# Last norm's vector turned through DRAM on GpSimd's queue, two constants loaded from GpSimd, and the first half's output in four pieces with banks of their own

## The chip, the cores and the metric

The kernel runs on one core of a Trainium2 chip. The metric is the device time of one execution in microseconds (us). The core has five engines with queues of their own: TensorE (PE, with its weight loads as PEld), VectorE (DVE), ScalarE (ACT), GpSimd (POOL) and SyncE (SP). Queues of SP, ACT and POOL also issue DMAs (in the profile SPq, ACTq and POOLq), which 16 DMA engines carry out. Matmul results land in PSUM, which has 8 banks of 128 x 512 numbers.

## What is computed

One decoder layer on 256 tokens of width 1024, in float32, with a final norm:

```python
mod = silu(c) @ w_ada + b_ada                       # 9 vectors of 1024: shifts, scales, gates
u = modulate(rmsnorm(h, norm_ff1), sh1, sc1)
h = h + 0.5 * g1 * swiglu(u, w_ff1_gate, w_ff1_up, w_ff1_down)
u = modulate(rmsnorm(h, norm_mix), sh2, sc2)
h = h + g2 * token_mixing(u, ...)                   # gated linear attention beside causal attention
u = modulate(rmsnorm(h, norm_ff2), sh3, sc3)
h = h + 0.5 * g3 * swiglu(u, w_ff2_gate, w_ff2_up, w_ff2_down)
return rmsnorm(h, norm_final)

def rmsnorm(x, g):
    return x * rsqrt(mean(x * x, axis=-1) + EPS) * g
```

The hidden width is 2816. The attention of the mixing stage adds a bias by distance, taken from a table `rel_bias` of 4 heads x 32 numbers.

## The kernel before

**Layout.** The activations `h` lie turned: features on the 128 partitions, in 8 blocks, tokens in the free dimension. All weights are loaded as 128 x 1024 pieces (512 KB) into 8 buffers called `raw` (line 186). Each piece is split into a rounded part `hi` (by ACT) and the rest `lo` (by DVE), 6 buffers each (line 193), and each product takes three matmuls (line 236). Nearly all matmuls are therefore of one form, 128 x 128 by 128 x 256.

**Stages.** First the *lead* (lines 327 to 775): the small vectors `colt` (line 328) and the input `x` are loaded, the input's norm is found (a root on POOL, line 425), and the first 32 pieces of weights come from one array, `in_first`, in the order of `LOADS` (line 25): for each of 8 blocks two pieces of the conditioning's weights, for DVE's dot products, and two of the first network's. Then the first feed-forward network, with the constants of the mixing stage loaded in between (`mix_constants`, line 793, at the fourth step); then the mixing stage, the second feed-forward network (line 1251), and the end (line 1260 on).

**Orders.** The order of ACT, DVE and PE is the order of the code (`in_order`, line 348), since each instruction is chained to the one before it on its engine. SP's and POOL's instructions aren't chained. Waits on data and on buffers are put in when the program is built.

**The constants of the mixing stage.** `mix_constants` loads `tri` into a `raw` buffer, then `mask` (128 x 448 integers), `rel` (the table of biases, 4 x 32) and `wlr_raw` (96 x 256), all from SP (line 796). On POOL, lines 803 to 807 fill a row `rrow` with a constant, copy 16 numbers of `rel` into it, and 16 more stretches (`BUCKETS`). Line 808 writes it to DRAM (`rdram`), and line 809 reads it back as `bias`, 128 x 4 x 256 numbers. `mask` and `bias` are used in the mixing stage.

**The two rows of gains.** The last two of the 8 feature blocks are computed with tokens on the partitions (`straight`), so the end needs two vectors as rows on all partitions. The gate's (`mods[:, 8, 6:8]`) is written from SBUF columns to DRAM on POOL's queue (`gdram`, line 1256), transposing on the way, and read back onto 128 partitions. The final norm's (`nf_row`, line 1258) is read from the end of `in_first`, where its 256 numbers stand as a row, by SP, into a buffer of `gqk`. `nf_row` is used at line 1320 alone.

**The end.** For each half `t` of the tokens `straight_products(t)` gives the last 256 columns; `summed(t)` adds up the squares of the first six blocks (a matmul with a column of ones), `squared(t)` (ACT) those of the last two, `root(t)` (DVE, then POOL) forms one over the root. `turn_out(t)` transposes six blocks of `h` into two banks, and `scaled` multiplies a piece by the root and issues its output: DVE's pieces of 256 columns from SP, ACT's pieces of 512 columns from ACT itself. `scaled_straight(t)` does the last 256 columns on DVE.

Of the kernel before, what the change touches and what calls it, by code (L numbers as in the profile page):

```python
# [10 lines left out]
F32 = mybir.dt.float32  # L11
F32R = mybir.dt.float32r
I32 = mybir.dt.int32
AF = mybir.ActivationFunctionType
ALU = mybir.AluOpType

P = 128
S = 256
D = 1024
# [54 lines left out]
TURNED, STRAIGHT = [0, 4, 2, 1, 5, 3], slice(6 * P, D)  # L74
# [13 lines left out]
C_BADA, C_N1, C_NM, C_N2, C_NF, C_C, C_GN = 0, 72, 80, 88, 96, 104, 112  # L88
# [3 lines left out]
def _places():  # L92

    places, at = {}, 0
    for piece in ["cols", "x0", "x1"] + LOADS.split():
        width = N_COLS if piece == "cols" else D + 2 if piece[0] == "a" else D
        places[piece] = at, width
        at += P * width
    places["nf"] = at, 2
    return places  # L100


FIRST = _places()


@with_exitstack
def hybrid_layer(ctx: ExitStack, tc: tile.TileContext, first, xT, tri_d, mask_d, rel_bias,
                 wlr, ada, gu1, dn1, win, gv, mv, gbr, wout, gu2, dn2, out):
    nc = tc.nc
# [5 lines left out]
    dr = ctx.enter_context(tc.tile_pool(name="dr", bufs=1, space=bass.MemoryType.DRAM))  # L115
# [24 lines left out]
    vec, act, ten = InOrder(nc.vector), InOrder(nc.scalar), InOrder(nc.tensor)  # L140
# [11 lines left out]
    def bank():  # L152
        return pp.tile([P, 512], F32, tag="b", name=name("b"), bufs=8)
# [15 lines left out]
    def row(shape=(P, S), dt=F32, tag="r1", bufs=6):  # L169
        return wk.tile(list(shape), dt, tag=tag, name=name(tag), bufs=bufs)  # L170

    def blk(i):
        return slice(i * P, (i + 1) * P)
# [618 lines left out]

    def mix_constants():
        ctri = load(tri_d)
        for to, src in ((mask, mask_d), (rel, rel_bias), (wlr_raw, wlr)):
            nc.sync.dma_start(to, src)
        act.activation(tri.rearrange("p a c -> p (a c)"), ctri[:, :4 * S], AF.Copy)

        act.activation(wlr_s, wlr_raw, AF.Copy)
        vec.tensor_tensor(out=wlr_s[64:96], in0=wlr_raw[64:96], in1=wlr_s[64:96], op=ALU.subtract)  # L800
        bank()

        nc.gpsimd.memset(rrow, NEG)
        nc.gpsimd.tensor_copy(rrow[:, 127:143], rel[:, :16])
        for bucket, first, last in BUCKETS:
            nc.gpsimd.tensor_copy(rrow[:, 127 + first:128 + last],
                                  rel[:, bucket:bucket + 1].to_broadcast([4, last - first + 1]))
        nc.gpsimd.dma_start(rdram, rrow)
        nc.gpsimd.dma_start(bias, bass.AP(tensor=rdram.tensor, offset=rdram[:, :].offset,
                                          ap=[[1, P], [NREL, 4], [1, S]]))  # L810

        vec.memset(glt.bitcast(F32), 0.0)
        vec.memset(glt[:, :, 16:81:64].bitcast(F32), 1.0)
# [419 lines left out]
    def first_product(i):  # L1233
# [3 lines left out]
        else:  # L1237
# [2 lines left out]
    play(START2, {"A": stream.more, "t": both_gates, "i": normed_part, "s": first_silu, "m": first_product,  # L1240
                  "r": lambda i: hid.add_rows(m[i], i), "o": lambda: low_last(sb[1], S, stream.take(), u3),
                  "g": lambda: next(steps), "H": lambda: rests.append(stream.high()), "L": lambda: rests.pop(0)()})
    def broadcast(src, at):
        t = row(tag="rbs" if at is None else "gqk", bufs=1 if at is None else 4)
        offset = src[:, :].offset if at is None else src.offset + at
        (nc.gpsimd if at is None else nc.sync).dma_start(t, bass.AP(tensor=src.tensor, offset=offset,
                                                                    ap=[[0, P], [1, 2 * P]]))
        return t

    dbanks = []  # L1250
    for at, (what, n) in enumerate(work2[3:-1]):
        pipe.run(gate_up(hid, u3) if what == "f" else down(n, dbanks, hid))
        slabs.step(Q3_AT.count(at))
        if at == 19:
            gdram = dr.tile([2, P], F32, name="gdram")
            nc.gpsimd.dma_start(gdram.rearrange("i p -> p i"), mods[:, 8, 6:8])
            stream.gains = broadcast(gdram, None)
            nf_row = broadcast(first, FIRST["nf"][0])

    bd = Boundary(8, h, lambda j: colt[:, C_NF + j:C_NF + j + 1], added=6, eps=D * EPS / P, order=TURNED)  # L1260
    bd.banks = dbanks
# [23 lines left out]
                    yield mm(b[:, :S], b, rows[:, i, r, blk(t)], ws_[i][part][:, wblk(6).start:wblk(7).stop],  # L1285
                             stop=(rows is hid.tiles[-1] and part == 1 and i == 1))

    ps, rs, cols = [bank(), bank()], [None, None], row((P, 8), tag="tiny", bufs=4)

    def summed(t):  # L1290
        part = bd.rms.parts[0]
        ten.matmul(ps[t][:, 0:1], part[:, blk(t)], ones[:, 0:1], start=True, stop=True)

    def squared(t):
        act.activation(row(tag="sq", bufs=4), straight[t][:, :S], AF.Square, scale=D ** -0.5, accum_out=cols[:, t:t + 1])

    def root(t):
        ms = row((P, 8), tag="tiny", bufs=4)
        vec.scalar_tensor_tensor(ms[:, :1], ps[t][:, 0:1], 1.0 / D, cols[:, t:t + 1], op0=ALU.mult, op1=ALU.add)
        rs[t] = inverse_root(ms, 1)  # L1300

    o = big().rearrange("p k s -> p (k s)")
    turned_o = {}

    def turn_out(t):
        turned_o[t] = [bank(), bank()]
        for j in (4, 5, 0, 1, 2, 3):
            ten.transpose(turned_o[t][j // 4][:, blk(j % 4)], h[:, j, blk(t)], ident)

    def scaled(engine, t, at, n):  # L1310
        src, dst = turned_o[t][at // 512][:, at % 512:at % 512 + n], o[:, t * D + at:t * D + at + n]
        if engine is act:
            act.activation(dst, src, AF.Copy, scale=rs[t][:, 0:1])
        else:
            vec.tensor_scalar(dst, src, rs[t][:, 0:1], None, op0=ALU.mult)
        (nc.scalar if engine is act else nc.sync).dma_start(out[blk(t), at:at + n], dst)  # L1316

    def scaled_straight(t):
        dst = o[:, t * D + 6 * P:(t + 1) * D]
        vec.scalar_tensor_tensor(dst, straight[t][:, :S], rs[t][:, 0:1], nf_row, op0=ALU.mult, op1=ALU.mult)  # L1320
        nc.sync.dma_start(out[blk(t), STRAIGHT], dst)

    all_of(straight_products(0))
    squared(0)
    for at, _ in enumerate(straight_products(1)):
        if at == 2:
            summed(0)
    root(0)
    squared(1)
    summed(1)  # L1330
    scaled_straight(0)
    turn_out(0)
    turn_out(1)
    scaled(vec, 0, 512, 256)
    root(1)
    scaled(act, 0, 0, 512)
    scaled_straight(1)
    scaled(vec, 1, 512, 256)
    scaled(act, 1, 0, 512)

def _c(a):
# [41 lines left out]
def _packed(i):  # L1385
    w = {k: np.asarray(v) for k, v in i.items()}
    d = {}
    x, pieces = _c(w["x"][0]), {}
    d["xT"] = _c(x.T.reshape(KD, P, S).transpose(1, 0, 2).reshape(P, KD * S))
    vec = [w["b_ada"][0], w["norm_ff1"][0], w["norm_mix"][0], w["norm_ff2"][0], w["norm_final"], w["c"][0],  # L1390
           w["gla_norm"][0]]
    pieces["cols"] = np.concatenate(vec).reshape(N_COLS, P).T
    pieces["x0"], pieces["x1"] = x[:P], x[P:]
    d["tri"], d["mask"] = _constants()
    d["rel_bias"] = _c(w["rel_bias"])
    d["wlr"] = np.zeros((3, 32, 256), np.float32)
    d["wlr"][:, :17] = np.concatenate([w["w_gla_lr"][0], w["b_gla_lr"]], 0)
    d["wlr"] = d["wlr"].reshape(96, 256)
    rows = w["w_ada"][0].T.reshape(9, KD, P, D)
    more = np.zeros((2, KD, P, 2), np.float32)  # L1400
    more[:, :, :, 0] = w["b_ada"][0].reshape(9, KD, P)[:2]
    more[1, :, :, 1] = 1.0
    adal = np.concatenate([rows[:2], more], 3)[::-1].transpose(1, 0, 2, 3)
    d["ada"] = _units(rows[2:].reshape(7 * KD, P, D))
    for n in ("1", "2"):
        g, u = (_col_tiles(w[f"w_ff{n}_{x}"][0]) for x in ("gate", "up"))
        both = np.stack([g, u], 2)
        if n == "1":
            lead = both[:LEAD].transpose(3, 1, 0, 2, 4).reshape(KD, P, 2, D)
            both = both[LEAD:]  # L1410
        d["gu" + n] = _c(both.reshape(len(both), P, 2048))
        d["dn" + n] = _row_units(w[f"w_ff{n}_down"][0])
    for k in range(KD):
        for i in range(2):
            pieces[f"a{k}{i}"], pieces[f"l{k}{i}"] = adal[k, i], lead[k, :, i]
    pieces["nf"] = w["norm_final"][6 * P:]
    d["first"] = np.concatenate([pieces[piece].reshape(-1) for piece in FIRST])
    wi = w["w_in"][0]
    at = np.cumsum([0, 256, 256, 512, 16, 512, 512, 512, 512, 1024, 1024])
    gq, gk, gv, glr, gog, mq, mk, mv, ga, gb = (wi[:, a:b] for a, b in zip(at[:-1], at[1:]))  # L1420
    d["win"] = _units(_col_tiles(np.concatenate([gk, gq, mk, mq, gog, ga], 1)))
    for n, m in (("gv", np.concatenate([gv, glr], 1)), ("mv", mv)):
        d[n] = _c(m.reshape(2, 4, P, -1).transpose(0, 2, 1, 3).reshape(2, P, -1))
    br = np.concatenate([_col_tiles(w["w_br_gla"][0]), _col_tiles(w["w_br_moba"][0])], 2)
    d["gbr"] = _c(np.stack([_col_tiles(gb), br], 2).reshape(KD, P, 2 * D))
    d["wout"] = _row_units(w["w_out"][0])
    return d
# [25 lines left out]
```

## Time and profile before

| what | value |
|---|---|
| three timed runs, median (lowest to highest) | 558.63 us (558.34 to 558.64) |
| the profiled execution | 559.21 us |
| its span, first to last instruction | 557.0 us |
| mean granted TensorE clock | 0.998 |
| instructions | 11698 |
| HBM read, written | 140.19 MB, 1.06 MB |

Times in views of the trace are microseconds from the start of the span. The profile is of one execution, so sums are made against its own time; it stands 0.58 us above the median of the timed runs. A row of a view by time gives start, length, engine, line of the kernel, operation, what is written and read by the program's names (`b` stands for several: PSUM banks and the large activations), and in brackets how long the engine sat idle before it, with what ended that. Most operations have line 132, which is a helper that issues them.

### The profile page before, as it was taken

How to read it: one execution, taken by the hardware profiler on the slowest of the kernel's cores; microseconds unless marked ns; L12 is line 12 of the kernel's file. 1: busy time of each engine (PE TensorE's matmuls, PEld its weight loads, DVE VectorE, ACT ScalarE, POOL GpSimd, SP SyncE). 2: the span in 40 equal slices, each digit the busy share in tenths (PEclk: the TensorE clock that was granted, in tenths of full speed). 3: DMA queues.
4: the chain of work that ended last, by engine and by line, in shares of the span. 5: the costliest groups of instructions: out<-in, count | busy, mean ns of one | idle time of the engine just before them, and what ended most of it. 6: DMA issues, size and time to landing. Idle time of an engine off the chain costs nothing.

```text
span 557.0 us, 11698 instructions
## 1 busy us (share of the span) xinstructions
PE 548.8 (99%) x4704; PEld 542.5 (97%) x4704; DVE 443.1 (80%) x695; ACT 305.3 (55%) x509; POOL 16.6 (3%) x37
## 2 busy tenths in 40 slices
PE   7999999999999999999999999999999999999996
PEld 5999999999999999999999999999999999999996
DVE  5999897788887897799998979899975556665555
ACT  5557754443445568953864543587554454455424
POOL 1000030000000100000001000000000000000000
PEclk9999999999999999999999999999999999999999
DMA  8999699999998626454589878834896566797102
GB/s 323 409 408 408 252 342 381 404 354 334 329 352 311 229 76 222 162 192 146 181 289 402 293 260 268 298 137 132 297 343 211 193 216 220 223 215 248 59 1 77
DMA packets 40750, 142.01 MB, mean 255 GB/s; under 512 B 4724, under 2 KB 6616, under 8 KB 40696
## 3 DMA queue, kind: packets, MB, share of 16 engines
q1 hardware_dynamic: 40008, 139.55, 70.4%
q10 hardware_dynamic: 432, 1.05, 0.5%
q8 instruction: 37, 0.61, 0.4%
q0 software_dynamic: 256, 0.66, 0.4%
q14 instruction: 17, 0.14, 0.1%
HBM read 140.19 MB, written 1.06 MB: 254 GB/s over the span
## 4 chain that ended last, share of the span: by engine, by line
PE 97%; DMA 2%; ACT 0%; SPq 0%; issue 0%; ACTq 0%
PE b L132 97%; DMA raw<-in_first 2%; ACT b L132 0%; SPq L190 0%; ACT hi L132 0%; SPq L331 0%; SPq L328 0%; ACTq L1316 0%; ACTq L132 0%
## 5 line engine op out<-in xcount | busy, mean ns | idle before, releaser
L132 PE MATMUL b<-ub,hi 128*128 128x256 f32 (+1 forms) x1920 | 318.5, 277 | 0.6 <-ACT hi L132 0.6
L132 PEld LDWEIGHTS b<-ub,hi 128*128 128x128 f32 x1920 | 280.7, 188 | 1.0 <-ACT hi L132 0.8
L132 DVE TENSOR_TENSOR lo<-raw,hi 128x1024 fp32r<-128x1024 f32 (+2 forms) x190 | 225.3, 1211 | 56.6 <-ACT hi L132 56.0
L132 PE MATMUL b<-ub,lo 128*128 128x256 f32 (+1 forms) x960 | 244.8, 277 | 0.0
L132 ACT ACTIVATE hi<-raw 128x1024 fp32r<-128x1024 f32 (+2 forms) x190 | 193.6, 1045 | 66.6 <-issue 29.9
L132 PEld LDWEIGHTS b<-ub,lo 128*128 128x128 f32 x960 | 170.9, 188 | 0.0
L132 PE MATMUL b<-s,hi 128*128 128x256 f32 x944 | 161.9, 276 | 0.0
L132 PEld LDWEIGHTS b<-s,hi 128*128 128x128 f32 x944 | 142.2, 188 | 0.0
L132 PE MATMUL b<-s,lo 128*128 128x256 f32 x472 | 130.3, 276 | 0.0
L132 PEld LDWEIGHTS b<-s,lo 128*128 128x128 f32 x472 | 88.6, 188 | 0.0
L132 DVE SCALAR_TENSOR_TENSOR raw<-raw,cact 128x1024 f32<-128x1024 f32 (+1 forms) x64 | 75.8, 1220 | 0.1
L132 ACT ACTIVATE s<-m 128x256 fp32r<-128x256 f32 x52 | 21.5, 417 | 81.6 <-DVE m L132 81.4
L132 ACT ACTIVATE sg<-b 128x256 f32<-128x256 f32 x46 | 17.3, 380 | 47.8 <-PE b L132 46.8
L132 DVE TENSOR_TENSOR s<-m,s 128x256 fp32r<-128x256 f32 x52 | 21.9, 424 | 20.6 <-ACT s L132 20.3
L132 DVE TENSOR_TENSOR m<-sg,b 128x256 f32<-128x256 f32 x43 | 17.8, 417 | 12.6 <-ACT sg L132 12.5
L132 ACT ACTIVATE s<-b 128x512 f32<-128x512 f32 (+5 forms) x38 | 14.7, 436 | 17.3 <-PE b L132 16.5
L132 PE MATMUL b<-hi,ub 128*128 128x264 f32 (+1 forms) x96 | 16.7, 323 | 0.0
L132 PEld LDWEIGHTS b<-hi,ub 128*128 128x128 f32 x96 | 13.9, 188 | 1.2
L425 POOL TENSOR_TENSOR tiny<-tiny,mhalf 128x2 f32<-128x2 f32 (+2 forms) x6 | 6.0, 1000 | 233.7 <-DVE tiny L132 233.7
L132 ACT ACTIVATE sq<-b 128x256 f32<-128x256 f32 x24 | 9.1, 405 | 6.3 <-DVE b L132 4.2
L132 DVE SCALAR_TENSOR_TENSOR b<-b,mods,b 128x256 f32<-128x256 f32 x24 | 10.3, 476 | 2.7 <-PE b L132 2.7
L132 ACT ACTIVATE ub<-n,mods 128x256 fp32r<-128x256 f32 x16 | 7.8, 508 | 8.0 <-DVE n L132 8.0
(141 smaller groups left out, 286.0 us busy)
## 6 DMA issues: line engine op xcount, KB each, us to landing
raw<-in_gu SPq DMA_DIRECT2D x72, 512.0 KB, 5.8
raw<-in_ada SPq DMA_DIRECT2D x56, 512.0 KB, 5.5
raw<-in_dn SPq DMA_DIRECT2D x44, 512.0 KB, 6.6
raw<-in_win SPq DMA_DIRECT2D x24, 512.0 KB, 4.4
raw<-in_first SPq DMA_DIRECT2D x16, 513.0 KB, 7.9
raw<-in_first SPq DMA_DIRECT2D x16, 512.0 KB, 7.8
raw<-in_gbr SPq DMA_DIRECT2D x16, 512.0 KB, 6.6
raw<-in_wout SPq DMA_DIRECT2D x8, 512.0 KB, 6.0
```

The costliest lines, as they stand in the source:

```text
L132: x = getattr(self.engine, op)(*args, **kw)
L425: nc.gpsimd.tensor_tensor(out=rs[:, :n], in0=ms[:, :n], in1=mhalf[:, :n], op=ALU.pow)
```

## The change

The final norm's two columns leave the array of the first loads; they are now written from `colt` in SBUF to DRAM and read back as a row, both on POOL's queue, by a function that also serves the gate's columns. `wlr_raw` is loaded by SP directly behind `tri`; `mask` and `rel` are loaded from POOL's queue. At the end both sums of squares share a bank; `turn_out` takes groups of blocks and gives each a bank of its own; ACT scales the first half's four blocks in two pieces of 256 columns, whose outputs SP issues; the first half's blocks 4 and 5 are turned ahead of the second half's sum, and the first half's sum comes two products earlier.

```diff
-    places["nf"] = at, 2
...
-        for to, src in ((mask, mask_d), (rel, rel_bias), (wlr_raw, wlr)):
-            nc.sync.dma_start(to, src)
+        nc.sync.dma_start(wlr_raw, wlr)
+        for to, src in ((mask, mask_d), (rel, rel_bias)):
+            nc.gpsimd.dma_start(to, src)
...
-    def broadcast(src, at):
-        t = row(tag="rbs" if at is None else "gqk", bufs=1 if at is None else 4)
-        offset = src[:, :].offset if at is None else src.offset + at
-        (nc.gpsimd if at is None else nc.sync).dma_start(t, bass.AP(tensor=src.tensor, offset=offset,
-                                                                    ap=[[0, P], [1, 2 * P]]))
+    def as_row(src, tag, bufs):
+        there, t = dr.tile([2, P], F32, name=f"{tag}_dram"), row(tag=tag, bufs=bufs)
+        nc.gpsimd.dma_start(there.rearrange("i p -> p i"), src)
+        nc.gpsimd.dma_start(t, bass.AP(tensor=there.tensor, offset=there[:, :].offset, ap=[[0, P], [1, 2 * P]]))
         return t
...
         if at == 19:
-            gdram = dr.tile([2, P], F32, name="gdram")
-            nc.gpsimd.dma_start(gdram.rearrange("i p -> p i"), mods[:, 8, 6:8])
-            stream.gains = broadcast(gdram, None)
-            nf_row = broadcast(first, FIRST["nf"][0])
+            stream.gains = as_row(mods[:, 8, 6:8], "rbs", 1)
+            nf_row = as_row(colt[:, C_NF + 6:C_NF + 8], "gqk", 4)
...
-    ps, rs, cols = [bank(), bank()], [None, None], row((P, 8), tag="tiny", bufs=4)
+    ps, rs, cols = bank(), [None, None], row((P, 8), tag="tiny", bufs=4)
...
-    def turn_out(t):
-        turned_o[t] = [bank(), bank()]
-        for j in (4, 5, 0, 1, 2, 3):
-            ten.transpose(turned_o[t][j // 4][:, blk(j % 4)], h[:, j, blk(t)], ident)
+    def turn_out(t, *parts):
+        for js in parts:
+            b = bank()
+            for i, j in enumerate(js):
+                ten.transpose(b[:, blk(i)], h[:, j, blk(t)], ident)
+            place[t, js] = b[:, :len(js) * P]
...
     for at, _ in enumerate(straight_products(1)):
-        if at == 2:
+        if at == 0:
             summed(0)
     root(0)
     squared(1)
+    turn_out(0, (4, 5))
     summed(1)
     scaled_straight(0)
-    turn_out(0)
-    turn_out(1)
-    scaled(vec, 0, 512, 256)
+    turn_out(0, (0, 1), (2, 3))
+    turn_out(1, (4, 5), (0, 1, 2, 3))
+    scaled(vec, nc.sync, 0, (4, 5))
     root(1)
-    scaled(act, 0, 0, 512)
+    scaled(act, nc.sync, 0, (0, 1))
+    scaled(act, nc.sync, 0, (2, 3))
     scaled_straight(1)
-    scaled(vec, 1, 512, 256)
-    scaled(act, 1, 0, 512)
+    scaled(vec, nc.sync, 1, (4, 5))
+    scaled(act, nc.scalar, 1, (0, 1, 2, 3))
...
-    pieces["nf"] = w["norm_final"][6 * P:]
```

More of the change, by code (lines that the diff above doesn't have):

```diff
@@ L1286, in straight_products @@
                              stop=(rows is hid.tiles[-1] and part == 1 and i == 1))
-    ps, rs, cols = [bank(), bank()], [None, None], row((P, 8), tag="tiny", bufs=4)
+    ps, rs, cols = bank(), [None, None], row((P, 8), tag="tiny", bufs=4)
     def summed(t):
         part = bd.rms.parts[0]
-        ten.matmul(ps[t][:, 0:1], part[:, blk(t)], ones[:, 0:1], start=True, stop=True)
+        ten.matmul(ps[:, t:t + 1], part[:, blk(t)], ones[:, 0:1], start=True, stop=True)
     def squared(t):
@@ L1298, in root, with written, scaled @@
         ms = row((P, 8), tag="tiny", bufs=4)
-        vec.scalar_tensor_tensor(ms[:, :1], ps[t][:, 0:1], 1.0 / D, cols[:, t:t + 1], op0=ALU.mult, op1=ALU.add)
+        vec.scalar_tensor_tensor(ms[:, :1], ps[:, t:t + 1], 1.0 / D, cols[:, t:t + 1], op0=ALU.mult, op1=ALU.add)
         rs[t] = inverse_root(ms, 1)
     o = big().rearrange("p k s -> p (k s)")
-    turned_o = {}
-    def turn_out(t):
-        turned_o[t] = [bank(), bank()]
-        for j in (4, 5, 0, 1, 2, 3):
-            ten.transpose(turned_o[t][j // 4][:, blk(j % 4)], h[:, j, blk(t)], ident)
-    def scaled(engine, t, at, n):
-        src, dst = turned_o[t][at // 512][:, at % 512:at % 512 + n], o[:, t * D + at:t * D + at + n]
+    place = {}
+    def turn_out(t, *parts):
[4 more added lines that the diff above has]
+            place[t, js] = b[:, :len(js) * P]
+    def written(queue, t, at, n):
+        queue.dma_start(out[blk(t), at:at + n], o[:, t * D + at:t * D + at + n])
+    def scaled(engine, queue, t, js):
+        at, n = js[0] * P, len(js) * P
+        dst = o[:, t * D + at:t * D + at + n]
         if engine is act:
-            act.activation(dst, src, AF.Copy, scale=rs[t][:, 0:1])
+            act.activation(dst, place[t, js], AF.Copy, scale=rs[t][:, 0:1])
         else:
-            vec.tensor_scalar(dst, src, rs[t][:, 0:1], None, op0=ALU.mult)
-        (nc.scalar if engine is act else nc.sync).dma_start(out[blk(t), at:at + n], dst)
+            vec.tensor_scalar(dst, place[t, js], rs[t][:, 0:1], None, op0=ALU.mult)
+        written(queue, t, at, n)
     def scaled_straight(t):
@@ L1320, in scaled_straight @@
         vec.scalar_tensor_tensor(dst, straight[t][:, :S], rs[t][:, 0:1], nf_row, op0=ALU.mult, op1=ALU.mult)
-        nc.sync.dma_start(out[blk(t), STRAIGHT], dst)
+        written(nc.sync, t, 6 * P, S)
     all_of(straight_products(0))
```

## The prediction

> **What bounds the kernel now.** I read the page's busy line first (busy us, share of the span, count), then the chain that ended last, in order of time (start, length, what).
>
> ```profile
> PE 548.8 (99%) x4704; PEld 542.5 (97%) x4704; DVE 443.1 (80%) x695; ACT 305.3 (55%) x509; POOL 16.6 (3%) x37
> ```
>
> ```profile
> 2.66 8.49 DMA raw<-in_first
> ...
> 11.85 539.40 PE b L132 x4658
> ```
>
> TensorE runs without a break from 11.85 to 551.25 us. So an edit between those two points costs or gains nothing unless it makes TensorE stop. What can be gained lies in the last 6 us; what can be lost lies ahead of 11.85, where a load of the first array ends the chain, and wherever loads come too late for TensorE. The stretches of the trace show where that is near:
>
> ```profile
> 14.00:46.00 32.00, 32.00 (x285) 32.00 (x284) 31.65 (x45) 18.80 (x26) 0.00 (x0) 1.00 1.03 409
> ...
> 60.00:70.00 10.00, 10.00 (x91) 10.00 (x90) 8.24 (x16) 7.13 (x12) 0.00 (x0) 1.00 0.55 181
> ...
> 492.00:498.00 6.00, 6.00 (x55) 6.00 (x54) 3.28 (x3) 2.56 (x4) 0.00 (x0) 1.00 0.97 64
> ```
>
> The columns are the stretch, its length, the busy time of PE, PEld, DVE, ACT and POOL, then clock, share of the DMA engines, GB/s. From 14 to 46 us the DMA engines are full (1.03, 409 GB/s) while PE is full too: the two are matched. At 60 to 70 us they are half idle. The third row is odd: full engines (0.97) that move 64 GB/s. I come back to it. How much room the matched stage has, shown at its fifth step (ACT's and PE's order of time):
>
> ```profile
> 31.95 1.06 ACT L132 ACTIVATE hi<-raw 128x1024 fp32r<-128x1024 f32 x1 [1.93 <-DMA raw<-in_first]
> 33.05 0.60 ACT L132 ACTIVATE ub<-b,gemv 128x256 fp32r<-128x256 f32 x1
> ```
>
> ```profile
> 34.74 1.07 PE L132 MATMUL b<-ub,hi 128*128 128x256 f32 x8
> ```
>
> ACT waits for the load (1.93 us), rounds it, then writes the next rows `ub`, done at 33.65; PE takes them at 34.74. A load that is late by more than 1.1 us stops PE here.
>
> **The change part by part.**
>
> *The end.* This is the order of time there:
>
> ```profile
> 550.84 0.48 DVE L132 TENSOR_SCALAR b<-b,tiny 128x256 f32<-128x256 f32 x1
> 551.24 0.15 DVE L132 SCALAR_TENSOR_TENSOR tiny<-b,tiny 128x1 f32<-128x1 f32 x1
> 551.35 0.34 SPq L1316 DMA_DIRECT2D out<-b  x1
> 551.36 0.69 ACT L132 ACTIVATE b<-b,tiny 128x512 f32<-128x512 f32 x1 [0.38 <-PE b L132]
> 551.54 0.55 POOL L425 TENSOR_TENSOR tiny<-tiny,mhalf 128x1 f32<-128x1 f32 x1 [1.30 <-DVE tiny L132]
> 552.07 0.34 ACTq L1316 DMA_DIRECT2D out<-b  x1
> ...
> 552.52 0.69 ACT L132 ACTIVATE b<-b,tiny 128x512 f32<-128x512 f32 x1 [0.48 <-POOL tiny L425]
> ...
> 552.64 0.33 SPq L1321 DMA_DIRECT2D out<-b  x1
> 553.06 0.41 SPq L1316 DMA_DIRECT2D out<-b  x1
> 553.24 0.34 ACTq L1316 DMA_DIRECT2D out<-b  x1
> ```
>
> And these are the DMA issues that the parts below need (count, size of one, us from issue to landing):
>
> ```profile
> bias<-rdram POOLq DMA_DIRECT2D x1, 512.0 KB, 7.9
> out<-b SPq DMA_DIRECT2D x4, 128.0 KB, 1.8
> out<-b ACTq DMA_DIRECT2D x2, 256.0 KB, 2.3
> mask<-in_mask SPq DMA_DIRECT2D x1, 224.0 KB, 4.9
> ...
> colt<-in_first SPq DMA_DIRECT2D x1, 56.5 KB, 3.4
> ...
> rdram<-wide POOLq DMA_DIRECT2D x1, 6.0 KB, 5.3
> gdram<-mods POOLq DMA_DIRECT2D x1, 1.0 KB, 10.6
> ```
>
> The root of the second half is ready at 551.54 + 0.55 = 552.09, yet ACT starts the last piece at 552.52, because its own queue issues the first half's output from 552.07 to 552.41. The change gives that issue to SP: 0.4 us, if ACT is free by then. ACT has two pieces of 256 columns in place of one of 512; 0.69 us becomes at most twice that, 1.38, if the width counted for nothing, and 0.69 if width were all. I take 0.85 in sum, nearer to the row. With banks of their own the first piece waits for four transposes and the sum of squares, not for six transposes, so it starts no later than 551.36: done near 552.2, against the root at 552.09. The root itself may come up to 0.15 earlier: the DVE step at 551.24 stands behind the piece of 550.84, whose two transposes now come first; how early its squares are there isn't quoted here, so I leave it at 0 to 0.15. SP's two new issues, 0.35 us each, fit between 551.69 and 552.64. One bank for both sums adds no wait: the read of the first sum is over well before the second is written. Value: the last issue goes from 553.24 to 552.8, **minus 0.4** (bounds: plus 0.4 if ACT's two pieces took 1.38 and SP's issues queued, minus 0.55). The landing behind it does not shrink: ACT's last transfer still lands last (552.8 + 2.3 against 553.0 + 1.8).
>
> *The queues.* The order on ACT, DVE and PE is written in the code. That on SP and POOL is not; it comes out of the build, and the trace shows by what rule:
>
> ```profile
> 0.92 0.41 POOL L803 MEMSET wide<- 4x384 f32 x1
> 1.37 0.28 POOL L335 TENSOR_SCALAR_AFFINE_SELECT ident<-ident 128x128 f32<-128x128 f32 x1
> 7.09 0.71 POOL L425 TENSOR_TENSOR tiny<-tiny,mhalf 128x2 f32<-128x2 f32 x1 [5.43 <-DVE tiny L132]
> 76.12 0.44 POOL L804 COPY wide<-rel 4x16 f32<-4x16 f32 x1 [68.32 <-DMA rel<-in_rel_bias]
> 76.51 4.44 POOL L806 COPY wide<-rel 4x3 f32<-4x3 f32 x16
> ...
> 293.07 2.55 POOL L425 TENSOR_TENSOR tiny<-tiny,mhalf 128x8 f32<-128x8 f32 x1 [93.77 <-DVE tiny L132]
> ...
> 486.91 0.76 POOL L1256 DMA_DIRECT2D gdram<-mods  x1 [111.52 <-DVE mods L132]
> ```
>
> ```profile
> 239.91 0.33 SPq L1246 DMA_DIRECT2D gqk<-in_first  x1
> ```
>
> Line 803 belongs to the constants of the mixing stage, whose copies run at 76 us, and runs at 0.92, ahead of line 335. Line 1246's second use stands after 1256 (486.91) and runs at 239.91, when a buffer of `gqk` came free. So an instruction goes out as soon as its input and its buffer are there and its engine idles. POOL idles for 5.4 us and then 68 us. Three DMAs of the change need nothing or only `colt`: `mask`, `rel` (0.5 KB, no cost of its own), and **the write of the last norm's two columns to DRAM**. I expect all three in the first microseconds.
>
> `mask`: 224 KB ahead of the first weights is 224/409 = **0.55 us** on the load that starts PE (0 if it comes later, 0.9 if its short rows cost more). The Trainium skill's "DMA: Bandwidth & Descriptors", "Issuing engines are not separate DMA queues", says the same against this edit: transfers of SP, ACT and GpSimd run on the same 16 engines and interleave, so another queue saves only issue time. No row of before tests that at the start.
>
> `bias` follows `rel` through line 806 and `rdram`, now in the matched stage: 512/409 = 1.25 us against 1.1 us of room: **0.2** (0 to 0.8).
>
> The write of the columns has the shape of `gdram<-mods`: two columns of 128 partitions, scattered as 256 single numbers, 1 KB. That DMA took 10.6 us from issue to landing, 5.3 more than the six times larger `rdram`, and in 492 to 498 us, just behind it, the engines were full and moved 64 GB/s in place of some 400: a hole of 6.0 x (1 - 64/409) = 5.1 us. PE didn't notice, since there loads run far ahead. In the first 46 us nothing runs ahead. The issue can follow `colt` (about 4 us), the hole then falls on the first weights or just after. Price: **4.5 us**, that is 5.1 less about half of the 1.1 us of room (0 if it goes out past 60 us or if the hole had another cause; 6.5 if it lasts as long as 492 to 498 and more). I take the near end of the hole because its own row is the only one of this shape. The gate's own write stays at 487 us. The skill's page named above, "Specifications", says that below 512 B the engines read, modify and write; that fits the row. By its fit in "Anatomy of one DMA — SWDGE (gpsimd) path" 1 KB would take 2.0 us, and the sum would be 2.5 us smaller; the row of 10.6 us differs, and it decides.
>
> The read-back into `gqk` waits for the buffer as the old load did, to about 240 us, now on POOL; the next root that could stand behind it there is that of 293.07: 0. SP loses three issues in stages where PE never stops: 0. `wlr` two issues earlier: 0, ACT uses it after `tri` anyway. The first array is 1 KB shorter: 0.
>
> Sum: -0.4 + 0.55 + 0.2 + 4.5 = **+4.85 us**. The profiled execution took 559.21 us (span 557.0 and 2.2 around it), so it would be 564.1. The three timed runs have a median of 558.63, 0.58 below it; taken from there the forecast is 563.5, with a range of its own of 560.5 to 566.
>
> **The rivals.**
>
> *The small write comes elsewhere* (not slower). Place: POOL's queue. If the build puts the write past 60 us, where the engines are half idle, or if the hole at 492 us isn't its doing, the 4.5 us fall away. For: `mask` and `rel`, which need nothing, did not go ahead of the weights on SP; so something can hold a ready DMA back. Against: SP had weights to load, POOL has nothing. It decides at slack: an 0.5 us hole is hidden, 2 us isn't. Time: 558.63 - 0.4 + 0 to 0.75 = 558.2 to 559.0.
>
> *The first root stands behind the table.* If `rel` lands before the squares are summed, the 17 copies (0.44 + 4.44 us) come before the root of 7.09 on POOL. By `rdram`'s 5.3 us `rel` lands near 7.5; the root would end near 7.5 + 4.9 + 0.7 = 13.1 in place of 7.80, and the products that need it,
>
> ```profile
> 8.73 2.51 PE L132 MATMUL b<-m,b 128*128 128x128 f32 x21
> ```
>
> which end 0.6 us ahead of 11.85, would start PE some 4.5 us later. Alone that gives 558.63 + 4.5 + 0.35 = 563.5; with half of the copies 561. Together with the hole it costs little more, as both hold the same start.
>
> *The change doesn't do what it says at the end*: ACT's two pieces eat the 0.4. It moves any case by 0.4 and decides nothing else.
>
> **How the numbers follow.** Hole in the first stage: 0.57. Small write elsewhere: 0.30. Root behind the table without the hole: 0.08. Something that I don't see and that gains: 0.05. 0.2% is 1.1 us, about what a measurement of this kernel can tell from no change. Slower: 0.57 + 0.08, less 0.02 for a hole that hides: 0.63. Same: 0.30 + 0.02 = 0.32. Faster: 0.05, since 0.4 us at the end is too little. The range from 558.1 to 565.5 takes in the rivals and leaves out the far end of the hole.
>
> **What would show it.** Right: POOL issues `mask`, `rel` and the small write in the first 10 to 20 us; a stretch there with full engines and far less than 400 GB/s; PE starts late or stops before 46 us; the small write lands 8 us or more after issue; after 540 us ACT's last piece stands right behind the root. Wrong: PE still starts near 11.9 and has no gap; then the time is 558.2 to 559.0. It would also be wrong if the write stands early and the bandwidth stays at 400.

## The result, and the profile after

| | median (lowest to highest), runs | ratio to before, 95% interval |
|---|---|---|
| before | 558.51 us (558.34 to 558.64), 4 | |
| changed | 566.30 us (565.72 to 567.13), 4 | 1.0141 [1.0123, 1.0158] |

The change costs 7.8 us. The forecast was 563.5 us, slower by 4.9, with a range that ended at 565.5: the sign and the place were right, the size was too small. The profiled execution took 565.72 us, its span 563.9 (before 557.0). Of all the executions reported below three were slow ones (569, 931 and 3179 us); the intervals leave them out, and without them no difference of medians changes by more than 0.08 us.

First the orders that the forecast named. POOL's order of time after (start, length, engine, line, operation):

```profile
1.31 0.71 POOL L796 DMA_DIRECT2D mask<-in_mask  x1 [0.33 <-issue]
...
7.28 0.72 POOL L424 TENSOR_TENSOR tiny<-tiny,mhalf 128x2 f32<-128x2 f32 x1 [4.86 <-DVE tiny L131]
7.97 0.57 POOL L796 DMA_DIRECT2D rel<-in_rel_bias  x1
...
8.90 0.75 POOL L1245 DMA_DIRECT2D gqk_dram<-colt  x1
...
13.31 4.29 POOL L806 COPY wide<-rel 4x3 f32<-4x3 f32 x16
17.89 0.54 POOL L808 DMA_DIRECT2D rdram<-wide  x1 [0.29 <-POOL wide L806]
26.20 0.79 POOL L809 DMA_DIRECT2D bias<-rdram  x1 [7.77 <-DMA rdram<-wide]
```

All three early DMAs are there by 9 us, and the first root (7.28) stands ahead of the table's copies, so the second rival, the root behind the table, did not happen. POOL sat idle for 4.86 us until the root could run, and `rel`, which needs nothing, went out only behind it: an instruction that is ready can stand behind one that isn't in the order that the build gave POOL. The small write is `gqk_dram<-colt`. Its row among the DMA issues (size, us to landing):

```profile
gqk_dram<-colt POOLq DMA_DIRECT2D x1, 1.0 KB, 11.2
```

So 1 KB takes 11.2 us to land. What the loads did meanwhile is in the stretches (length; busy PE, PEld, DVE, ACT, POOL; granted clock; share of the DMA engines; GB/s):

```profile
14.00:18.00 4.00, 4.00 (x36) 3.88 (x34) 1.68 (x3) 0.15 (x1) 3.71 (x17) 1.00 1.39 177
18.00:22.00 4.00, 0.07 (x1) 0.00 (x0) 1.60 (x3) 1.45 (x2) 0.43 (x1) 0.80 0.66 129
22.00:26.00 4.00, 3.85 (x18) 3.85 (x19) 3.61 (x6) 1.53 (x3) 0.00 (x0) 0.50 1.03 409
26.00:30.00 4.00, 4.00 (x32) 4.00 (x32) 3.66 (x8) 2.60 (x4) 0.79 (x1) 0.84 1.03 417
```

The hole lies from 14 to 22 us. At 409 GB/s those 8 us would have moved 3.27 MB; they moved 4 x 177 + 4 x 129 = 1.22 MB. The lost 2.05 MB are 5.0 us of loads at that rate. ACT, DVE and then PE pay for it (ACT's, DVE's and PE's orders of time, in this sequence):

```profile
20.55 1.06 ACT L131 ACTIVATE hi<-raw 128x1024 fp32r<-128x1024 f32 x1 [6.40 <-DMA raw<-in_first]
```

```profile
19.91 1.23 DVE L131 SCALAR_TENSOR_TENSOR raw<-raw,cact 128x1026 f32<-128x1026 f32 x1 [4.24 <-DMA raw<-in_first]
```

```profile
17.01 1.07 PE L131 MATMUL b<-ub,lo 128*128 128x256 f32 x8
22.15 2.08 PE L131 MATMUL b<-ub,hi 128*128 128x256 f32 x8 [4.07 <-ACT ub L131]
24.02 1.91 PE L131 MATMUL b<-ub,lo 128*128 128x256 f32 x8
25.73 3.63 PE L131 MATMUL b<-ub,hi 128*128 128x256 f32 x24
29.20 1.07 PE L131 MATMUL b<-ub,lo 128*128 128x256 f32 x8
...
62.75 0.39 PE L131 MATMUL b<-ub,hi 128*128 128x256 f32 x2
```

PE stops for 4.07 us. Then 24 products take 3.63 us where such a group takes 2.88 at a clock of 1.00 (31.92 to 34.80 in this profile); the granted clock is 0.50 and then 0.84. The product that opens the next stage stands at 62.75; before it stood here:

```profile
56.50 0.39 PE L132 MATMUL b<-ub,hi 128*128 128x256 f32 x2
```

That is 6.25 us, nearly the whole loss, all of it made ahead of 30 us. The profile offers two readings. One: 4 us of waiting and 2.5 us of slow clock. The other: 5 us of lost loads in a stage that lives off its loads, and then something smaller. The experiments decide between them.

The end, in SP's and ACT's orders of time and, as the third row, the one DMA issue from 559.5 to 559.9 us:

```profile
556.94 2.89 SPq L1310 DMA_DIRECT2D out<-b  x6
```

```profile
557.46 1.56 ACT L131 ACTIVATE b<-b,tiny 128x256 f32<-128x256 f32 x3
559.05 0.35 ACTq L1310 DMA_DIRECT2D out<-b  x1
```

```profile
out<-b SPq DMA_DIRECT2D x1, 128.0 KB, 3.2
```

ACT's last issue now follows its last piece at once, as forecast (557.46 + 1.56 = 559.02). But SP issues six times in one stretch, 2.89/6 = 0.48 us each, and its last output takes 3.2 us to land, where an output of this size took 1.8 before. What is moved from 560.4 to 560.85 us shows part of why, by the queues (packets, MB, share of the engines):

```profile
q10 hardware_dynamic: 89, 0.18, 102.5%
q1 hardware_dynamic: 2, 0.00, 0.2%
```

q10 is ACT's queue, q1 SP's: ACT's 256 KB have the engines almost to themselves in this stretch, while SP's last piece waits.

### The profile page after: what moved, and what is told of

It reads as the page before. It is cut to its first block, busy times and chain, and to the rows that moved or that the text cites. A ratio compares the mean times of both kernels' runs of the same rounds, so it can differ in the third digit from the quotient of the medians.

```text
span 563.9 us, 11707 instructions
## 1 busy us (share of the span) xinstructions
PE 552.1 (98%) x4704; PEld 545.5 (97%) x4704; DVE 443.2 (79%) x695; ACT 305.1 (54%) x510; POOL 18.7 (3%) x41
## 4 chain that ended last, share of the span: by engine, by line
PE 95%; DMA 3%; ACT 0%; DVE 0%; issue 0%; POOLq 0%; DVEq 0%; SPq 0%
PE b L131 95%; DMA raw<-in_first 3%; DMA b<-in_first 1%; ACT hi L131 0%; POOLq L1451 0%; ACT ub L131 0%; DVE b L131 0%; DVEq L1451 0%; SPq L189 0%; DVE tiny L131 0%; POOLq L424 0%
## 5 line engine op out<-in xcount | busy, mean ns | idle before, releaser
L131 DVE TENSOR_TENSOR m<-sg,b 128x256 f32<-128x256 f32 x43 | 17.8, 417 | 12.6 <-ACT sg L131 12.5
```

Source lines behind the costliest of these rows:

```text
L131: x = getattr(self.engine, op)(*args, **kw)
```

## The experiments

Sixteen kernels were run. "+" is the difference in us of the median to that of the runs of the kernel before that were made beside them (558.37 to 558.53 us). Differences under about 0.2% are within what can be told from none.

| kernel | us | + | ratio, 95% interval |
|---|---|---|---|
| new end alone | 558.93 | 0.42 | 1.0012 [1.0003, 1.0021] |
| constants alone | 559.39 | 0.88 | 1.0017 [1.0008, 1.0026] |
| row through DRAM alone | 565.05 | 6.54 | 1.0120 [1.0106, 1.0134] |
| whole change, row written late | 560.49 | 1.98 | 1.0036 [1.0023, 1.0048] |
| whole change, PE kept busy in the wait | 566.34 | 7.81 | 1.0140 [1.0126, 1.0153] |
| 1 KB as four rows | 558.61 | 0.08 | 1.0000 [0.9991, 1.0009] |
| 256 numbers, 512 bytes apart | 558.55 | 0.02 | 1.0000 [0.9991, 1.0009] |
| the same, 64 bytes apart | 558.42 | 0.05 | 1.0001 [0.9992, 1.0010] |
| the same, 16 bytes apart | 558.53 | 0.11 | 1.0006 [0.9997, 1.0015] |
| the same, 8 bytes apart | 560.38 | 1.86 | 1.0031 [1.0020, 1.0042] |
| the same, touching | 564.81 | 6.29 | 1.0112 [1.0097, 1.0127] |
| 128 pairs, touching | 560.45 | 1.93 | 1.0035 [1.0021, 1.0049] |
| before, one issue from SP | 558.39 | -0.14 | 1.0000 [0.9991, 1.0009] |
| constants alone, bias late | 558.41 | 0.04 | 1.0001 [0.9992, 1.0010] |
| new end with three pieces | 558.21 | -0.16 | 0.9998 [0.9989, 1.0006] |
| whole change, three prices out | 558.80 | 0.38 | 1.0007 [0.9997, 1.0016] |

### The parts one by one

Each of the three parts was put alone into the kernel before. In the diffs below "..." stands for lines that are not shown. The end:

```diff
...
-    turn_out(0)
-    turn_out(1)
-    scaled(vec, 0, 512, 256)
+    turn_out(0, (0, 1), (2, 3))
+    turn_out(1, (4, 5), (0, 1, 2, 3))
+    scaled(vec, nc.sync, 0, (4, 5))
     root(1)
-    scaled(act, 0, 0, 512)
+    scaled(act, nc.sync, 0, (0, 1))
+    scaled(act, nc.sync, 0, (2, 3))
...
```

> The kernel before with the changed end alone; the final norm's row and the constants load as before. The prediction's sum gives -0.4 us: 558.1. Rival, read from the profile after (from the last product to the span's end 7.15 us against 6.59 before): SP's six issues in a row make the last output land later, +0.5 us: 559.0. Neither theory expects a hole or a stop of TensorE before 550 us.

Measured: 558.93 us, 0.42 slower. The new end does not gain; it costs.

The constants:

```diff
-        for to, src in ((mask, mask_d), (rel, rel_bias), (wlr_raw, wlr)):
-            nc.sync.dma_start(to, src)
+        nc.sync.dma_start(wlr_raw, wlr)
+        for to, src in ((mask, mask_d), (rel, rel_bias)):
+            nc.gpsimd.dma_start(to, src)
```

> The kernel before with mask and rel on GpSimd's queue alone. If the small scattered write is the cause, this is within 0.6 us of 558.5 and TensorE starts near 11.3 to 12.4 us without a stop. Rival: the constants' transfers in the first 40 us (mask 224 KB, bias 512 KB) starve the weights: then TensorE stops before 46 us and the time is 561 to 565.

Measured: 559.39 us, 0.88 slower. PE starts in time, but stops at 40 us. Its order of time, and ACT's ahead of it:

```profile
40.89 1.22 PE L132 MATMUL b<-ub,hi 128*128 128x256 f32 x8 [0.95 <-ACT ub L132]
```

```profile
39.28 1.06 ACT L132 ACTIVATE hi<-raw 128x1024 fp32r<-128x1024 f32 x1 [4.09 <-DMA raw<-in_first]
```

ACT waits 4.09 us for a load of weights; the 512 KB of `bias`, issued at 29 us, are the transfer put between.

The row:

```diff
...
-            nf_row = broadcast(first, FIRST["nf"][0])
+            nf_row = as_row(colt[:, C_NF + 6:C_NF + 8], "gqk", 4)
...
```

> The kernel before with the final norm's row written to DRAM and read back on GpSimd's queue, alone. Small write as the cause: packets near 12 to 14 us, then some 6 us of DMA engines that hardly move, TensorE stops about 4 us and then runs at half clock for some 3 us more: 564.5 to 566. Rival (constants are the cause): 558.5.

Measured: 565.05 us, 6.54 slower. The three parts add up to 0.42 + 0.88 + 6.54 = 7.84 us; the whole change costs 7.79. So they account for it, and the row is five sixths of it.

The whole change with the row's write late (its source is a copy that DVE makes at the step where the gate's columns are written):

```diff
+            late = row((P, 2), tag="late", bufs=1)
+            vec.tensor_copy(late, colt[:, C_NF + 6:C_NF + 8])
-            nf_row = as_row(colt[:, C_NF + 6:C_NF + 8], "gqk", 4)
+            nf_row = as_row(late, "gqk", 4)
```

> The whole change, but the small write takes its two columns from a copy that DVE makes in its order at the twentieth step of the second network (about 487 us), so the write can't go out earlier. Small write as the cause: the hole moves to about 490 to 505 us, where it is hidden; 558.1 to 559.2, by what the new end is worth. Rival: constants or the end are the cause: 561 or more.

Measured: 560.49 us. The write itself is no cheaper there:

```profile
gqk_dram<-late POOLq DMA_DIRECT2D x1, 1.0 KB, 12.5
```

It takes 12.5 us, and the loads again fall off behind it (4 us from 504 us on):

```profile
504.00:508.00 4.00, 4.00 (x38) 4.00 (x37) 2.75 (x3) 1.53 (x3) 0.00 (x0) 1.00 1.39 192
```

But PE is busy for 4.00 of 4.00 us there: what the hole costs hangs on where it falls. The end and the constants alone make 0.42 + 0.88 = 1.30 of the 1.98 us that are left; the rest lies within the interval (1.0023 is 1.3 us).

### Is it the clock or the loads?

Nine full-precision products of zeros, added to a sum that is open, stand ahead of the step that stalls (in the changed kernel):

```diff
+FILL = 9
...
+    def fill():
+        for _ in range(FILL):
+            mm(lead_banks[0][:, :S], lead_banks[0], zeros[:, :P], zeros[:, :S])
...
```

> The changed kernel with nine more TensorE products of 128x256 in full fp32 (zeros added to a sum, so the values stay as they are) put just ahead of the step that stalls; nothing else differs. Theory: of the 6.3 us that TensorE is late at the end of the first stage, 4.1 us are the wait for the loads and about 2.5 us are products that run at a granted clock of 0.50 and 0.84 after that wait. Work in the wait keeps the clock up: the stretch 22 to 30 us then shows a clock near 1.00, and the time is about 563.8 us, 2.5 us under the changed kernel's 566.3. Rival: what is slow behind the wait is the data that comes late (the hi and lo parts), not the clock; then the clock may stay up but the time does not fall (566 us), or it rises by the 3 to 4 us of the added products if these do not fit in the wait.

Measured: 566.34 us, no gain against 566.30, where I had expected 2.5 us. The stretches and PE's order of time:

```profile
22.00:26.00 4.00, 4.00 (x36) 4.00 (x35) 2.30 (x5) 1.17 (x2) 0.57 (x1) 1.00 1.03 413
26.00:30.00 4.00, 3.24 (x26) 2.87 (x25) 3.96 (x8) 2.71 (x4) 0.23 (x1) 1.00 1.03 417
```

```profile
17.61 4.05 PE L132 MATMUL b<-wide 128*128 128x256 f32 x18
...
26.91 1.22 PE L132 MATMUL b<-ub,lo 128*128 128x256 f32 x8 [0.29 <-DVE lo L132]
28.60 1.16 PE L132 MATMUL b<-ub,hi 128*128 128x256 f32 x8 [0.47 <-DVE ub L132]
...
35.10 1.22 PE L132 MATMUL b<-ub,hi 128*128 128x256 f32 x8 [0.80 <-ACT ub L132]
...
62.55 0.39 PE L132 MATMUL b<-ub,hi 128*128 128x256 f32 x2
```

The fill (18 matmuls in the trace, two for each product) takes the wait's place, the clock stays at 1.00, and PE still opens the next stage at 62.55 (62.75 with the slow clock). It now stops for data instead, at 26.91, 28.60 and 35.10. My theory of the clock falls for the whole change: PE ran slowly through products whose data would not have come sooner. The loads set the time here, and the engines move at full rate again from 22 us on in both kernels. The fill was not put into the kernel with the row alone.

### What in the small write makes the hole?

The next kernels are the kernel before with one more write of 1 KB, read by nothing, that POOL issues right behind the first root. Only the shape differs:

```diff
+            scrap = dr.tile([4, 64], F32, name="scrap")
+            nc.gpsimd.dma_start(scrap, colt[:4, :64])
```

> The kernel before with one early write of 1 KB to DRAM from GpSimd's queue, right behind the first root, of the same size as the new small write, but as four rows of 256 bytes in place of 256 single numbers (the written rows are read by nothing). Theory: the hole in the loads comes from the 256 scattered numbers, so there is none here: 558.5 us, and the stretch 14 to 22 us keeps about 410 GB/s. Rival: any write to DRAM that GpSimd issues among the loads makes the hole, whatever its shape: about 565 us.

```diff
+            scrap = dr.tile([2 * P, P], F32, name="scrap")
+            nc.gpsimd.dma_start(scrap.rearrange("(i p) c -> p i c", i=2)[:, :, 0:1], colt[:, C_NF + 6:C_NF + 8, None])
```

> The kernel before with one early write of 256 single numbers of 4 bytes from GpSimd's queue, right behind the first root, as the new small write is, but each number 512 bytes from the next in DRAM in place of next to it (read by nothing). It tells two theories of the hole apart. If the hole comes from 256 writes of 4 bytes as such, it is here too: about 565 us with under 200 GB/s in the stretch 14 to 22 us. If it comes from many such writes to the same few stretches of memory, one behind the other, it is gone: about 558.5 us, and the write lands in under 8 us where the changed kernel's took 11.2.

The same with `[2 * P, 16]`, 64 bytes from number to number:

> The run with 256 single numbers 512 bytes apart (558.55 us, no hole, landed 5.4 us after its issue), but with the numbers 64 bytes apart. If what makes the hole is that numbers share a stretch of memory shorter than 64 bytes, there is none here either: 558.5 us and a landing under 6 us. If the stretch that they must not share is longer (512 bytes hold 8 of these numbers, against 128 in the changed kernel), part of the hole is back: 559.5 to 565 us, landing in 6 to 11 us.

With `[2 * P, 4]`, 16 bytes:

> The runs with 256 single numbers 512 and 64 bytes apart (no hole, landing 5.4 us), with the numbers 16 bytes apart. Theory: the hole comes from numbers that share a stretch of 64 bytes (four do here, 16 in the changed kernel): a part of the hole is back, 559.5 to 563 us, with a landing of 6 to 11 us. Rival: only numbers that touch, as rows of one array do, make it: 558.4 us and a landing under 6 us.

With `[2 * P, 2]`, 8 bytes:

> The same write with the numbers 8 bytes apart. At 16 bytes there was no hole (558.53 us) and a landing of 6.0 us where 64 and 512 bytes gave 5.4. If the price grows step by step as more numbers share a stretch of memory, it lies between: 559 to 562 us, landing in 6.5 to 9 us. If only numbers that touch make the hole: 558.5 us and a landing near 6 us.

Touching, as in the changed kernel:

```diff
+            scrap = dr.tile([2, P], F32, name="scrap")
+            nc.gpsimd.dma_start(scrap.rearrange("i p -> p i"), colt[:, C_NF + 6:C_NF + 8])
```

> The control of the three runs with spread numbers: the kernel before with the same early write of 256 single numbers, touching one another in two rows of 128 as the changed kernel's new small write has them, but read by nothing, and all else as before. Theory: that the numbers touch is what makes the hole: about 565 us, a landing of 11 us and under 200 GB/s in the stretch 14 to 22 us. Rival: the hole needs something else that the changed kernel does with that row (its place in DRAM, or the norm's row gone from the first array): 558.5 us and a landing under 6 us.

And touching, but as 128 pairs of 8 bytes, not transposed:

```diff
+            scrap = dr.tile([P, 2], F32, name="scrap")
+            nc.gpsimd.dma_start(scrap, colt[:, C_NF + 6:C_NF + 8])
```

> The same 1 KB without the transposing: each partition writes its two numbers side by side, 128 writes of 8 bytes that touch one another (a row that could be read with a step of two). If many small writes to the same stretch make the hole, half as many make about half of it: 560 to 563 us, landing in 7 to 9 us. If it comes from the order of the transposed write, in which two rows are written in turn, there is none: 558.5 us.

The times are in the table. These are the stretch 14 to 18 us (12 to 22 for the touching numbers) and the issue's row, of the kernels with 64 bytes, 16 bytes, 8 bytes, touching numbers, and pairs, in this order:

```profile
14.00:18.00 4.00, 4.00 (x38) 4.00 (x37) 3.91 (x7) 2.68 (x4) 0.00 (x0) 1.00 1.03 416
```

```profile
scrap<-colt POOLq DMA_DIRECT2D x1, 1.0 KB, 5.4
```

```profile
14.00:18.00 4.00, 4.00 (x37) 4.00 (x37) 3.91 (x8) 2.67 (x4) 0.00 (x0) 1.00 1.01 375
```

```profile
scrap<-colt POOLq DMA_DIRECT2D x1, 1.0 KB, 6.0
```

```profile
14.00:18.00 4.00, 3.68 (x33) 3.48 (x31) 2.51 (x5) 0.80 (x1) 0.00 (x0) 1.00 0.95 259
```

```profile
scrap<-colt POOLq DMA_DIRECT2D x1, 1.0 KB, 7.6
```

```profile
12.00:14.00 2.00, 2.00 (x20) 2.00 (x19) 0.58 (x1) 1.62 (x3) 0.00 (x0) 1.00 2.22 298
14.00:18.00 4.00, 3.45 (x30) 3.26 (x29) 2.44 (x3) 0.00 (x0) 0.00 (x0) 1.00 0.61 122
18.00:22.00 4.00, 0.54 (x5) 0.34 (x3) 1.86 (x3) 1.72 (x3) 0.00 (x0) 0.78 0.81 188
```

```profile
scrap<-colt POOLq DMA_DIRECT2D x1, 1.0 KB, 11.4
```

```profile
14.00:18.00 4.00, 3.90 (x33) 3.55 (x31) 3.81 (x6) 1.19 (x2) 0.00 (x0) 1.00 0.96 179
```

```profile
scrap<-colt POOLq DMA_DIRECT2D x1, 1.0 KB, 7.7
```

The price comes in by steps. As four rows, or as single numbers 64 or 512 bytes apart, 1 KB lands in 5.3 to 5.4 us and costs nothing that can be measured. At 16 bytes the landing takes 6.0 us and the stretch dips a little (375 GB/s), again with no loss of time that can be measured. At 8 bytes it takes 7.6 us and costs 1.86 us, when the numbers touch 11.4 us and 6.29. Half as many writes, of 8 bytes, cost 1.93, a third. That is also what the 256 numbers at 8 bytes cost (1.86, with 7.6 us to landing against 7.7), so in these two runs the distance from write to write counts and not the number of writes. So the rival that only touching numbers make a hole falls, and so does the one that needs the transposed order; my theory that it is enough for numbers to share a stretch of 64 bytes falls too, since four in one did no harm that can be measured. A price that grows with the writes in the same few bytes fits all these runs; how long that stretch is they do not show. What follows: 128 or 256 small writes from POOL's queue, 8 bytes or less from one to the next in DRAM, hold up the loads of SP's queue too. By which mechanism, the runs do not show.

### The other two prices

`bias` late: the kernel with the constants alone, but POOL fills the table from a copy of `rel` that DVE makes at the fourth step of the first network.

```diff
...
+        vec.tensor_copy(late, rel)
...
-        nc.gpsimd.tensor_copy(rrow[:, 127:143], rel[:, :16])
+        nc.gpsimd.tensor_copy(rrow[:, 127:143], late[:, :16])
...
```

> The run of the constants alone (559.39 us, 0.88 over before), but POOL fills the table from a copy of rel that DVE makes at the fourth step of the first network, so the table, its write and the 512 KB read of bias come at about 76 us, where the kernel before has them; mask and rel still load in the first 15 us. Theory: the first stage lives off loads that run at 404 to 414 GB/s all along, so each load put into it costs its bytes; bias is 512 KB, 1.28 us at 409 GB/s, mask 224 KB, 0.56 us. Without bias in the stage the time falls by about 0.7 us, to 558.5 to 558.9. Rival: the 0.88 us are mask's, or the order of wlr and mask on SP's queue: the time stays at 559.2 to 559.5.

Measured: 558.41 us, 0.04 over before. So `bias` makes the 0.88 us of the constants; `mask`, `rel` and the order of `wlr` cost nothing that can be measured (by the interval -0.4 to 0.6 us), though `mask` still loads in the first stage.

The new end alone with three pieces (the diff is against the new end), and the kernel before with one issue moved from ACT to SP:

```diff
-    turn_out(0, (0, 1), (2, 3))
+    turn_out(0, (0, 1, 2, 3))
...
-    scaled(act, nc.sync, 0, (0, 1))
-    scaled(act, nc.sync, 0, (2, 3))
+    scaled(act, nc.sync, 0, (0, 1, 2, 3))
```

> The run of the new end alone (558.93 us, 0.42 over before), but the first half's output in three pieces: ACT's four blocks in one bank, one operation and one 256 KB output issued by SP. Order of sums and turns and the shared bank stay as in the new end. Theory: the new end loses by the split, since its 128 KB pieces with rows of 1 KB move at about 260 GB/s where the 256 KB pieces move at 370, and SP has one issue more: 558.3 to 558.6 here. Rival: it loses by the new order (blocks turned ahead of the second sum, or the earlier first sum): still 558.9.

```diff
...
-    scaled(act, 0, 0, 512)
+    scaled(act, 0, 0, 512, nc.sync)
```

> The kernel before with one edit: the first half's 256 KB piece of the output that ACT writes and issues is issued by SP; pieces and banks stay. Theory: what the new end had right is that ACT's issue of 0.34 us leaves the path of ACT's last piece (its last issue came 2.30 us behind the last product in place of 2.83); what it lost is that SP has two more issues of 0.4 us and the last piece stands behind the others. With one issue moved and 2 KB rows kept, the last issue comes 0.3 to 0.4 us earlier: 558.1 to 558.3 us. Rival: the output's transfers, not the issues, set the end, or SP's own last issue is pushed back: 558.5 to 558.9 us.

Measured: 558.21 us with three pieces (-0.16) and 558.39 us with the one issue moved (-0.14); neither can be told from no change. The fourth piece is most likely what the end loses by: 0.58 us lie between four and three pieces, whose intervals overlap a little. My reason for it in the expectation, rows of 1 KB that move at 260 GB/s, is doubtful. SP issues one piece of 131 kB per 0.48 us, which by itself is 272 GB/s, and in the stretches of the changed kernel the outputs ran so until ACT's transfer came in:

```profile
559.00:560.00 1.00, 0.00 (x0) 0.00 (x0) 0.18 (x1) 0.03 (x1) 0.00 (x0) 1.00 0.79 263
560.00:561.00 1.00, 0.00 (x0) 0.00 (x0) 0.00 (x0) 0.00 (x0) 0.00 (x0) 1.00 0.99 366
```

The engines are not full (0.79) while SP issues. The pieces themselves are done only every 0.4 to 0.6 us, and SP's issues follow them by 0.03 us at first and by 0.25 at the end (559.17 and 559.42). So the pace of the pieces and of the issues would explain the lower rate without the rows; no run parts these.

The whole change without the three prices: late row, late bias, three pieces.

> The whole change with its three prices taken out: the small write's source is copied by DVE at the step where the gate's columns are written (as in the run with the late row), the table is filled from a late copy of rel (as in the run with the late bias), and the first half's output has three pieces (as in the run with the three pieces). If the parts add up as the single runs did (late row and rest 2.0 over before, less 0.9 for bias and 0.6 for the fourth piece), this comes to 558.4 to 559.0 us. If something in the whole costs that no part shows, it is above 559.2.

Measured: 558.80 us, ratio 1.0007 [0.9997, 1.0016]. Nothing of weight is left over. No version ran measurably faster than the kernel before.

## Why the prediction was right and wrong

**Right: where and which.** The forecast put the loss on the small write early in the first stage, on its hole in the loads, and on PE stopping ahead of 46 us; the row alone and the touching numbers alone show each of these. It was right that such a hole costs nothing that can be measured late in the kernel, where PE has its data in hand (4.00 of 4.00 us busy from 504 to 508 us). The first rival (the write comes late) is what the run with the late row made true by hand; its 558.2 to 559.0 us were not reached (560.49), since the constants and the end cost 1.30. The second (root behind the table) did not occur. Of the rule for POOL's queue, "as soon as its input and its buffer are there and its engine idles", `rel` is a counterexample: it went out at 7.97 us, behind the root that POOL waited for.

**Wrong: the size of the small write.** The step was "Price: 4.5 us, that is 5.1 less about half of the 1.1 us of room". The touching numbers alone cost 6.29 us, by the interval 5.4 to 7.1; the loads they lose in 12 to 22 us are 2 x 111 + 4 x 287 + 4 x 221 kB, at 409 GB/s 5.5 us. So 5.1 for the hole was a fair reading. The room was read at the wrong place: 1.1 us is that of the fifth step, and PE stops at the second. There, in the kernel before, the rows `ub` are done at 17.41 + 0.60 = 18.01 and PE takes them at 18.42, which leaves 0.4 us (ACT's and PE's orders of time):

```profile
17.41 0.60 ACT L132 ACTIVATE ub<-b,gemv 128x256 fp32r<-128x256 f32 x1
```

```profile
18.42 1.07 PE L132 MATMUL b<-ub,hi 128*128 128x256 f32 x8
```

The room grows by some 0.3 us from step to step, to 2.0 us at the eighth (49.06 and 51.06), since the four loads of a step are 2.10 MB, 5.1 us at 409 GB/s, while PE's step takes 5.44 us (18.42 to 23.86). That gives nothing back after a stop: PE is full, and what it has lost it can't make up.

The bytes less the 0.4 us explain 5.1 of 6.29 us, and the lower end of the interval is 5.4; what the rest is stays open. Part of it may be the low clock. With touching numbers alone PE does not stop again after 21.89 us (granted clock 0.50 from 22 to 26 us, 0.87 from 26 to 30), and at the fourth step it takes the rows 1.08 us after they are done, at 33.69 + 0.60 = 34.29 (ACT's and PE's orders of time):

```profile
33.69 0.60 ACT L132 ACTIVATE ub<-b,gemv 128x256 fp32r<-128x256 f32 x1 [0.46 <-DVE raw L132]
```

```profile
35.37 1.07 PE L132 MATMUL b<-ub,hi 128*128 128x256 f32 x8
```

In the whole change, where `bias` is among the loads, the same product comes only 0.27 us after its rows (34.69 + 0.59 = 35.28):

```profile
34.69 0.59 ACT L131 ACTIVATE ub<-b,gemv 128x256 fp32r<-128x256 f32 x1
```

```profile
35.55 1.07 PE L131 MATMUL b<-ub,hi 128*128 128x256 f32 x8
```

So a faster clock had little to gain there, as the fill showed; in the kernel with the touching numbers alone it may cost up to 1.08 us, and no run tests that. The forecast's aside "the sum would be 2.5 us smaller" took a time to landing for a price: 1 KB of numbers 64 bytes apart takes 5.4 us to land and costs nothing that can be measured.

**Wrong: the sign of the end.** The step was "SP's two new issues fit between 551.69 and 552.64" and with it "ACT's last transfer still lands last". ACT's last issue did come at once behind its last piece, and ACT's first two pieces took about 0.87 us together, as forecast (1.56 for three, of which the third took 0.69). But SP's last of six issues became the one that lands last, 3.2 us after its issue. In place of minus 0.4 the end costs 0.42. That is the size of the bound of plus 0.4, by one half of its reason: SP's last issue came 0.25 us after its piece was done, and its transfer took 1.4 us longer than such a transfer did before.

**Mask and bias, right in sum only.** Forecast 0.55 for `mask` and 0.2 for `bias`; measured about 0 (by the interval up to 0.6) and 0.88. Together the two bring 1.8 us of transfer and cost 0.88, so here the room did take a part: before, at the step where PE stops with the constants alone (40.89 us), it is 1.4 us (38.74 and 40.18). In the whole change `bias` falls behind the hole (26.20 us) and, by the sum of the parts, costs the same.

**The sum.** -0.4 + 0.55 + 0.2 + 4.5 = 4.85 against 0.42 + 0.88 + 6.54 = 7.84: of the 3 us missing, 2 are the small write and 0.8 the end.

The Trainium skill's "DMA: Bandwidth & Descriptors", "Specifications", which the forecast drew on, says that transfers below 512 bytes read, modify and write. No run shows whether this makes the price; by itself it does not, since 256 numbers of 4 bytes, 16 bytes or more apart, are below 512 bytes too and cost nothing that can be measured.

## What to carry to other kernels

In a stage that keeps the DMA engines and TensorE full, price lost or added bytes by bytes over the measured rate, and take off only the room of the very step that they hit: here it was 0.4 us at the second step and 2.0 at the eighth. Turning a column into a row by a write of touching numbers to DRAM is dear wherever loads are short. Write it where loads run ahead, or spread the numbers (the runs tested the spread write, not a read of it), and let the source's last writer decide when it goes out, since a DMA whose source is ready early can go out early: here at 8.90 us, for a row that is used at the end. At the end of a kernel count the issues of each queue to the last one's landing: a piece split to free one engine can make the other queue's last transfer the end.

## What the runs showed of the hardware

Writing 256 numbers of 4 bytes from GpSimd's queue took 11.4 us when they touched and 5.4 us when they lay 64 bytes apart, and of these two only the former held up other transfers: the stretch 14 to 18 us moved 122 GB/s against 416. After PE's wait of 4.07 us in the changed kernel the granted clock was 0.50 for the next 4 us and 0.84 in the 4 us behind them; after one of 1.13 us (numbers 8 bytes apart) it stayed at 1.00:

```profile
18.81 1.21 PE L132 MATMUL b<-ub,hi 128*128 128x256 f32 x8 [1.13 <-ACT ub L132]
```

```profile
18.00:22.00 4.00, 3.19 (x26) 3.19 (x27) 3.71 (x5) 2.20 (x4) 0.00 (x0) 1.00 1.03 397
```

The Trainium skill's "TensorE: Matmul & The Clock Gate", "Part 1: The HAM clock gate (the "warmup" mystery)", gives half rate after an idle window of about 3.4 us and full rate after as long a busy one; the traces agree (0.50 behind 4.07 us of idling, 1.00 behind 1.13, and 1.00 again within 8 us of the restart). The run with the fill shows that in the whole change, short of data, this costs no time that can be measured.
